# One layer of a streaming encoder: 64-row score products filled up to 128 rows, and a tile of the down projection split later

## The chip, the core and the metric

The kernel runs on one core of a Trainium2 chip. The metric is the device time of one execution in microseconds (us), as the median of several runs. The core has a matrix engine, TensorE (PE in the rows, its weight loads PEld), VectorE (DVE), ScalarE (ACT), GpSimd (POOL) and a queue (SP) that issues most of the DMAs. Each engine works through its own queue in order; semaphores tie the queues together.

## The reference, cut to what matters

512 positions of width 1024 go through one residual block: a normalised input is projected, eight heads of forgetting attention and eight latent heads of attention work on it, their outputs are gated, summed and projected, and a SwiGLU feed-forward part with 2816 hidden features and a last normalisation follow. The two places that matter here:

```python
def latent_attention(q_nope, q_rope, k_nope, k_rope, v):      # 8 heads, nope 64, rope 32, blocks of 128 queries
    s = (jnp.einsum('bqhd,bkhd->bhqk', qn, k_nope, preferred_element_type=jnp.float32)
         + jnp.einsum('bqhr,bkr->bhqk', qr, k_rope, preferred_element_type=jnp.float32))
    s = jnp.where(k_chunk[None, :] <= q_chunk[:, None], s * scale, NEG_INF)
    p = jax.nn.softmax(s, axis=-1).astype(v.dtype)
    return jnp.einsum('bhqk,bkhd->bqhd', p, v)

def swiglu(xn, w_gate, w_up, w_down):
    return (jax.nn.silu(xn @ w_gate) * (xn @ w_up)) @ w_down
```

## The kernel before

Every fp32 operand is held as two fp32r parts, a high and a low one (`split`, L98: ScalarE rounds to the high part, VectorE subtracts for the low part), and a product is made of three matmuls, high by high, high by low and low by high (`mm3`, L124). TensorE's own instructions are pinned in program order; the order of the other queues is set by a planner when the kernel is built (`schedule_with_timeline_sim`, L1042).

Attention runs over 64 items: for the latent heads ("b", tiles `hb`) and then the forgetting heads ("a", tiles `ha`), eight heads each, and for each head four blocks of 128 queries. The item of block i covers 128 (i + 1) keys, so the score products are 128, 256, 384 or 512 columns wide. The loop at L847 issues the scores three items ahead (`scores`, L641, tile `sp`); then come the maximum and the exponential (`softmax_a`, L653, tile `pe`), the scaling by the reciprocal of the sum (`softmax_b`, L663, L666 on VectorE), the transposes of the scaled block (`transpose`, L671, tile `pt`, then `pth` and `ptl`), and after the last item of a head the product with the values (`values`, tile `py`). Between these steps a `Filler` (L783) puts the matmuls of other jobs into TensorE's queue in a fixed list (L822): gate projections (`gates`, tile `pg`), the projections of later heads (`project_b`, tiles `pqb`, `pkb`; `project_a`, tile `pqa`), values (`pva`) and branch projections (`pb`). Each job that reads weights has them split just before (`whi` on ScalarE at L101, `wlo` on VectorE at L102).

`project_b(j)` (L566) makes the tiles of two latent heads. A head's tile `hd` has four planes of 128 rows by 512 positions. With `own` for the 64 rows of this head (rows 0 to 63 for even heads, 64 to 127 for odd ones) and `oth` for the other 64: plane 0 holds the query's high part in `own` and its low part in `oth`; plane 1 holds the key's high part in both halves; plane 2 holds the key's low part in `own`, and its other half is never written; plane 3 holds the rotary parts. The tiles come from a ring of 17 buffers (`u8`), so a later head's tile may have to wait until an earlier tile was read for the last time. Scores of a latent item are three matmuls into one bank: plane 0 by plane 1 over 128 rows (high by high and low by high at once), plane 0 by plane 2 over the 64 rows `own` (high by low, L650), and plane 3 by the shared rotary key `krs` over 100 rows. Scores of a forgetting item are two matmuls, over 128 and 70 rows.

GpSimd does the minimum in the gates (L435), a small copy into each `hb` tile (L590), and small memsets and DMAs for the `ha` tiles (L614 to L617).

The down projection (L955 on) has two halves of 512 output columns. In each half eleven strips of weights (256 hidden features, so two steps of 128 each) are added into one PSUM bank for each of the four tiles of 128 positions; the last three strips run tile by tile, so that the tail of one tile (adding the residual, squares, scaling, storing) runs beside the matmuls of the next. In the second half the last tile of positions is two parts of 256 columns in two banks, in all eleven strips.

Of the kernel before, what the change touches and what calls it, by code (L numbers as in the profile page):

```python
# [8 lines left out]
F32 = mybir.dt.float32  # L9
# [3 lines left out]
AF = mybir.ActivationFunctionType  # L13
ALU = mybir.AluOpType
AX = mybir.AxisListType

P = 128
D = 1024
S = 512
NT = S // P  # L20
# [4 lines left out]
NHC = HID // P  # L25
# [41 lines left out]
def tile_hybrid_fox_mla_block(  # L67
# [6 lines left out]
    nc = tc.nc  # L74
# [11 lines left out]
    def u8(shape, dtype, name):  # L86
        return big.tile(shape, dtype, name=name, tag="u8", bufs=17)

    def small(shape, name, dtype=F32, bufs=2):
        return big.tile(shape, dtype, name=name, tag=name, bufs=bufs)  # L90

    def tmp(shape, name, dtype=F32):
        return big.tile(shape, dtype, name=name, tag="p", bufs=4)

    def bank(tag, name):
        return ps.tile([P, 512], F32, name=name, tag=tag, bufs=3 if tag == "a" else 5)

    def split(hi, lo, src, scale=None):  # L98

        if scale is None:  # L100
            one = nc.scalar.copy(out=hi, in_=src)  # L101
            two = nc.vector.tensor_tensor(out=lo, in0=src, in1=hi.bitcast(F32), op=ALU.subtract)  # L102
        else:
            one = nc.scalar.activation(out=hi, in_=src, func=AF.Copy, scale=scale)
            two = nc.vector.scalar_tensor_tensor(out=lo, in0=src, scalar=scale, in1=hi.bitcast(F32),
                                                 op0=ALU.mult, op1=ALU.subtract)
        if pin[1]:
            tc.keep_in_program_order(one)
            tc.keep_in_program_order(two)
# [4 lines left out]
    def matmul(*args, **kw):  # L114
        ins = nc.tensor.matmul(*args, **kw)  # L115
        if pin[0]:
            tc.keep_in_program_order(ins)
# [6 lines left out]
    def mm3(o, a, b, start, stop):  # L124

        matmul(o, lhsT=a[0], rhs=b[0], start=start, stop=False)
        matmul(o, lhsT=a[0], rhs=b[1], start=False, stop=False)
        matmul(o, lhsT=a[1], rhs=b[0], start=False, stop=stop)

    def weights(src, a, b, spare=False):  # L130

        raw = big.tile([P, a, b], F32, name="wraw", tag="wr", bufs=2)
        nc.sync.dma_start(out=raw, in_=src)
        return split_weights(raw, spare)
# [23 lines left out]
    def mean4(out, ss, width):  # L158

        nc.vector.tensor_scalar(out=out, in0=ss, scalar1=-4.0 / width, scalar2=-4.0 * EPS, op0=ALU.mult, op1=ALU.add)  # L160

    def mean_rsqrt(parts, width, name, out=None):

        m = small([P, 1], name + "_m")
        mean4(m, parts[0], width)
        for p_ in parts[1:]:
            nc.vector.scalar_tensor_tensor(out=m, in0=p_, scalar=-4.0 / width, in1=m, op0=ALU.mult, op1=ALU.add)
        return rsqrt(m, 1, name, out)
# [17 lines left out]
    c1 = big.tile([P, C_INVF], F32, name="c1", tag="c1", bufs=1)  # L186
# [137 lines left out]
    for st in "f0 k0 f1 t0 k1 f2 t1 f3 t2 m1 t3 f4 t4 m2 t5 f5 f6 t6 f7 m3 t7 w0 w1".split():  # L324
        n = int(st[1])
# [50 lines left out]
    for n, (t, k, p_) in enumerate(jobs):  # L376
        if n == 72:
            token_rms()
        matmul(pms[t][:, :MISCW], lhsT=xt(k, slice(t * P, (t + 1) * P))[p_ == 2],
               rhs=(mh, ml)[p_ == 1][k // 4][:, k % 4, :], start=(k, p_) == (0, 0), stop=(k, p_) == (KC - 1, 2))  # L380
# [98 lines left out]
    def step():  # L479

        for _ in range(next(stages, 0)):
            next(pre, None)
# [41 lines left out]
    for t in range(NT):  # L524
        cols = slice(t * P, (t + 1) * P)
# [40 lines left out]
    def project_b(j):  # L566

        cols = slice(j * P, (j + 1) * P)
        two = [u8([P, 4, S], F32R, f"hb{2 * j + e}") for e in range(2)]
        pq = bank("b" if j == 0 else "a", "pqb")  # L570
        for k in range(2):
            mm3(pq, (qn[:, 0, k, cols], qn[:, 1, k, cols]), (cq[:, 0, k, :], cq[:, 1, k, :]), k == 0, k == 1)
            yield
        pk_ = bank("b" if j == 0 else "a", "pkb")
        mm3(pk_, (kvs[:, 2, cols], kvs[:, 3, cols]), (kvs[:, 0, :], kvs[:, 1, :]), True, True)
        yield
        if j == 0:
            rotated_to_features()
        for e in range(2):
            h = 2 * j + e  # L580
            hd = two[e]
            own, oth = slice(64 * e, 64 * e + 64), slice(64 - 64 * e, 128 - 64 * e)
            split(hd[own, 0, :], hd[oth, 0, :], pq[own, :], scale=SCALE_B)
            split(hd[own, 1, :], hd[own, 2, :], pk_[own, :])
            nc.scalar.copy(out=hd[oth, 1, :], in_=pk_[own, :])
            rows = slice(h % 4 * ROPE, (h % 4 + 1) * ROPE)
            nc.vector.tensor_copy(out=hd[0:32, 3, :], in_=qrh[h // 4][rows, :])
            nc.vector.tensor_copy(out=hd[32:64, 3, :], in_=qrl[h // 4][rows, :])
            nc.scalar.copy(out=hd[64:96, 3, :], in_=qrh[h // 4][rows, :])
            nc.gpsimd.tensor_copy(out=hd[96:100, 3, :], in_=qrow)  # L590
            heads["b", h] = hd
            yield
# [48 lines left out]
    def scores(it):  # L641
        b, h, W, qc = it.b, it.h, it.W, it.qc
        hd = heads[b, h]
        sp = it.sp = bank("b", "sp")
        matmul(sp[:, :W], lhsT=hd[:, 0, qc], rhs=hd[:, 1, :W], start=True, stop=False)
        if b == "a":
            matmul(sp[:, :W], lhsT=hd[0:70, 2, qc], rhs=hd[0:70, 3, :W], start=False, stop=True)
        else:
            own = slice(64 * (h % 2), 64 * (h % 2) + 64)
            matmul(sp[:, :W], lhsT=hd[own, 0, qc], rhs=hd[own, 2, :W], start=False, stop=False)  # L650
            matmul(sp[:, :W], lhsT=hd[0:100, 3, qc], rhs=krs[0:100, :W], start=False, stop=True)

    def softmax_a(it):  # L653
# [222 lines left out]
    gf = u8([P, 2, D], F32, "gf")  # L876
# [3 lines left out]
    def hrow(t):  # L880
        return ha[t // 2][:, t % 2, :]
# [9 lines left out]
    for half in range(2):  # L891
# [11 lines left out]
        for t in range(NT):  # L903
            po = bank("a", "po")
            cols = slice(t * P, (t + 1) * P)
# [7 lines left out]
            jk = tmp([P, S], "jk")  # L913
            nc.scalar.activation(out=jk, in_=hrow(t)[:, nn], func=AF.Square, accum_out=ssh[:, 2 * t + half:2 * t + half + 1])
            nc.vector.tensor_tensor(out=hn[t][:, nn], in0=hrow(t)[:, nn], in1=gf[:, 0, nn], op=ALU.mult)
            if half == 1:
                r = mean_rsqrt([ssh[:, 2 * t:2 * t + 1], ssh[:, 2 * t + 1:2 * t + 2]], D, "nh")
# [4 lines left out]
    act = [u8([P, 2, 2, S], F32R, f"act{i}") for i in range(NHC // 2)]  # L922
# [12 lines left out]
    for s in range(NHC // 2):  # L935
# [11 lines left out]
        for e in range(2):  # L947
            sg = tmp([P, S], "sg")
            last = nc.scalar.activation(out=sg, in_=pg[e], func=AF.Silu)
# [5 lines left out]
    ssf = small([P, 2 * NT + 1], "ssf", bufs=1)  # L955
    for half in range(2):
        nn = slice(half * 512, (half + 1) * 512)

        parts = [(t, 0, 512) for t in range(NT)]
        if half == 1:  # L960
            parts[-1:] = [(NT - 1, 0, 256), (NT - 1, 256, 512)]
        po = [bank("b" if half == 0 or t == NT - 1 else "a", "pd") for t, _, _ in parts]

        def step(s, e, n, w):
            t, c0, c1 = parts[n]
            cols = slice(t * P, (t + 1) * P)
            mm3(po[n][:, 0:c1 - c0], (act[s][:, e, 0, cols], act[s][:, e, 1, cols]),
                (w[0][:, e, c0:c1], w[1][:, e, c0:c1]), s == 0 and e == 0, s == NHC // 2 - 1 and e == 1)

        def load(s):  # L970
            return weights(w_ffn_down[s * 256:(s + 1) * 256, nn].rearrange("(k p) n -> p k n", p=P), 2, 512)

        last = 3
        for s in range(NHC // 2 - last):
            w = load(s)
            for e in range(2):
                for n in range(len(parts)):
                    step(s, e, n, w)
        ws = [(s, load(s)) for s in range(NHC // 2 - last, NHC // 2)]
        for n, (t, c0, c1) in enumerate(parts):  # L980
            for s, w in ws:
                for e in range(2):
                    step(s, e, n, w)
            cols = slice(half * 512 + c0, half * 512 + c1)
            hv = hrow(t)[:, cols]
            nc.vector.tensor_tensor(out=hv, in0=po[n][:, 0:c1 - c0], in1=hv, op=ALU.add)
            jk = tmp([P, S], "jk")
            at = 2 * t + half + (c0 > 0)
            nc.scalar.activation(out=jk[:, 0:c1 - c0], in_=hv, func=AF.Square, accum_out=ssf[:, at:at + 1])
            nc.vector.tensor_tensor(out=hv, in0=hv, in1=gf[:, 1, cols], op=ALU.mult)  # L990
            if half == 1 and c1 == 512:
                r = mean_rsqrt([ssf[:, i:i + 1] for i in range(2 * t, at + 1)], D, "nf")
                rows = slice(t * P, (t + 1) * P)
                h0, h1 = hrow(t)[:, 0:384], hrow(t)[:, 384:1024]
                nc.scalar.activation(out=h0, in_=h0, func=AF.Copy, scale=r)
                nc.vector.tensor_scalar(out=h1, in0=h1, scalar1=r, scalar2=None, op0=ALU.mult)
                nc.sync.dma_start(out=out2[rows, :], in_=hrow(t))
# [55 lines left out]
```

## Time and profile before

| | |
|---|---|
| median of 3 runs | 749.67 us (748.59 to 749.82) |
| profiled execution, time | 749.56 us |
| its span, first to last instruction | 747.8 us |
| TensorE busy | 730.3 us of the span |
| VectorE busy | 423.0 us |
| ScalarE busy | 335.9 us |
| GpSimd busy | 72.0 us |
| mean granted TensorE clock | 0.993 of full |
| latent scores, first to last start | 72.1 to 182.6 us |
| down projection, first to last matmul | 619.7 to 740.7 us |

The span is what the profiler saw from the first to the last instruction; the execution's time has 1.8 us around it. Busy time of TensorE counts matmuls that overlap, with ends that are modelled; what a matmul costs is read from the distance between the starts of one and the next. "idle before <-" names what ended an engine's idle time; "issue" is time in which the engine waited for nothing that the profile shows.

### The profile page before, as it was taken

To read this page: it belongs to the slowest core of one execution; us is meant where nothing else is said; L and a number is where in the kernel's file an instruction comes from. 1 tells how busy PE (TensorE), PEld (TensorE's weight loads), DVE (VectorE), ACT (ScalarE), POOL (GpSimd) and SP (SyncE) were. 2 spreads that over 40 slices of the span, in tenths; PEclk is the share of its full clock that TensorE was granted. 3 is DMA by queue.
4 is the path that set the end of the run, shared out by engine and by line. 5 is a ranking of instruction groups with operands and counts; after the bars stand their busy time and mean duration, and the time that the engine had idled before them with its cause. 6 is when DMAs were issued, how large, how long until landed. Compare 5 with 4: busy or idle time off the path is not lost.

```text
span 747.8 us, 9512 instructions
## 1 busy us (share of the span) xinstructions
PE 730.3 (98%) x3601; PEld 608.4 (81%) x3601; DVE 423.0 (57%) x818; ACT 335.9 (45%) x635; POOL 72.0 (10%) x88
## 2 busy tenths in 40 slices
PE   5999999999999999999999999999999999999996
PEld 3988777878888888887899888888888888888885
DVE  6998988666898986576644332333333233225214
ACT  7457977555675774534514232323232232213113
POOL 4242331012121020300000000000000000000000
PEclk9899999999999999999999999999999999999999
DMA  8512112131223222274302323333332323323212
GB/s 280 170 45 69 41 49 57 29 86 30 87 58 78 65 57 85 86 244 148 114 29 86 112 85 108 90 93 104 87 111 85 112 86 96 102 85 112 85 57 112
DMA packets 68941, 69.45 MB, mean 93 GB/s; under 512 B 3808, under 2 KB 58352, under 8 KB 68896
## 3 DMA queue, kind: packets, MB, share of 16 engines
q1 hardware_dynamic: 66240, 64.91, 29.3%
q10 hardware_dynamic: 1824, 3.38, 1.4%
q0 software_dynamic: 832, 0.57, 0.3%
q8 instruction: 28, 0.46, 0.2%
q14 instruction: 17, 0.14, 0.1%
HBM read 66.59 MB, written 2.10 MB: 92 GB/s over the span
## 4 chain that ended last, share of the span: by engine, by line
PE 90%; DVE 4%; ACT 2%; DMA 2%; issue 1%; SPq 0%
PE pg L115 26%; PE pd L115 16%; PE pu L115 16%; PE pqa L115 6%; PE pb L115 6%; PE sp L115 4%; PE po L115 4%; PE pva L115 3%; PE py L115 3%; PE pt L120 2%; PE pm L115 2%; DMA wraw<-in_w_out_dram 1%; DMA wraw<-in_w_in_dram 1%; PE pqb L115 1%; ACT sq L340 1%
## 5 line engine op out<-in xcount | busy, mean ns | idle before, releaser
L102 DVE TENSOR_TENSOR wlo<-wraw,whi 128x1024 fp32r<-128x1024 f32 x102 | 125.4, 1230 | 200.6 <-ACT whi L101 200.1
L101 ACT CAST whi<-wraw 128x1024 fp32r<-128x1024 f32 x102 | 106.8, 1048 | 214.4 <-PE pu L115 78.5
L115 PE MATMUL pd<-whi,act 128*128 128x512 f32 (+1 forms) x396 | 110.9, 366 | 0.0
L115 PEld LDWEIGHTS pd<-whi,act 128*128 128x128 f32 x396 | 71.6, 189 | 12.4
L115 PE MATMUL pd<-wlo,act 128*128 128x512 f32 (+1 forms) x198 | 72.5, 366 | 0.0
L115 PE MATMUL pg<-hTh,wlo 128*128 128x512 f32 (+1 forms) x192 | 71.4, 372 | 0.0
L115 PE MATMUL pu<-hTl,whi 128*128 128x512 f32 (+1 forms) x192 | 71.3, 371 | 0.0
L115 PE MATMUL pu<-hTh,whi 128*128 128x512 f32 (+1 forms) x192 | 71.3, 371 | 0.0
L115 PE MATMUL pu<-hTh,wlo 128*128 128x512 f32 (+1 forms) x192 | 71.3, 371 | 0.0
L115 PE MATMUL pg<-hTl,whi 128*128 128x512 f32 (+1 forms) x192 | 71.3, 371 | 0.0
L115 PE MATMUL pg<-hTh,whi 128*128 128x512 f32 (+1 forms) x192 | 71.1, 371 | 0.0
L115 PE MATMUL pg<-xTh,whi 128*128 128x512 f32 x128 | 52.4, 410 | 0.0
L115 PE MATMUL pg<-xTh,wlo 128*128 128x512 f32 x128 | 50.2, 392 | 0.0
L115 PE MATMUL pg<-xTl,whi 128*128 128x512 f32 x128 | 50.1, 391 | 0.0
L115 PEld LDWEIGHTS pd<-wlo,act 128*128 128x128 f32 x198 | 37.4, 189 | 6.1
L115 PEld LDWEIGHTS pu<-hTh,wlo 128*128 128x128 f32 x192 | 36.2, 188 | 6.3
L115 PEld LDWEIGHTS pg<-hTh,wlo 128*128 128x128 f32 x192 | 36.2, 188 | 6.3
L115 PEld LDWEIGHTS pu<-hTl,whi 128*128 128x128 f32 x192 | 36.2, 188 | 6.3
L115 PEld LDWEIGHTS pg<-hTl,whi 128*128 128x128 f32 x192 | 36.2, 188 | 6.2
L115 PEld LDWEIGHTS pg<-hTh,whi 128*128 128x128 f32 x192 | 36.2, 188 | 6.2
L115 PEld LDWEIGHTS pu<-hTh,whi 128*128 128x128 f32 x192 | 36.2, 188 | 6.1
L435 POOL TENSOR_SCALAR gate<-gate 128x512 f32<-128x512 f32 x16 | 28.2, 1762 | 116.8 <-ACT gate L433 116.5
(281 smaller groups left out, 1433.7 us busy)
## 6 DMA issues: line engine op xcount, KB each, us to landing
wraw<-in_w_in_dram SPq DMA_DIRECT2D x28, 512.0 KB, 3.9
wraw<-in_w_ffn_gate_dram SPq DMA_DIRECT2D x22, 512.0 KB, 3.7
wraw<-in_w_ffn_up_dram SPq DMA_DIRECT2D x22, 512.0 KB, 3.7
wraw<-in_w_ffn_down_dram SPq DMA_DIRECT2D x22, 512.0 KB, 3.7
wraw<-in_w_out_dram SPq DMA_DIRECT2D x8, 512.0 KB, 4.0
xf<-in_xT_dram SPq DMA_DIRECT2D x8, 256.0 KB, 5.1
wraw<-in_w_branch_b_dram SPq DMA_DIRECT2D x4, 512.0 KB, 3.5
wraw<-in_w_branch_a_dram SPq DMA_DIRECT2D x4, 512.0 KB, 3.3
```

Source lines behind the costliest of these rows:

```text
L101: one = nc.scalar.copy(out=hi, in_=src)
L102: two = nc.vector.tensor_tensor(out=lo, in0=src, in1=hi.bitcast(F32), op=ALU.subtract)
L115: ins = nc.tensor.matmul(*args, **kw)
L120: ins = nc.tensor.transpose(*args)
L340: tc.keep_in_program_order(nc.scalar.activation(out=dst, in_=src, func=AF.Square))
L435: nc.gpsimd.tensor_scalar(out=g, in0=g, scalar1=1e30, scalar2=None, op0=ALU.min)
```

## The change

The unused half of plane 2 of each latent head's tile is set to zero by GpSimd, and the second score product runs over all 128 rows instead of 64: the added rows multiply the query's low part by zero. In the down projection's second half, the last tile of positions is one bank of 512 columns for the first eight strips. In the last three strips columns 0 to 255 go on in that bank, and then columns 256 to 511 of these three strips are added up in a new bank, `late`. The first bank's columns 256 to 511 are added to the residual by an instruction of its own, and the new bank's columns after it. All other tiles do what they did.

```diff
@@ project_b
             split(hd[own, 0, :], hd[oth, 0, :], pq[own, :], scale=SCALE_B)
+
+            nc.gpsimd.memset(hd[oth, 2, :].bitcast(F32), 0.0)
             split(hd[own, 1, :], hd[own, 2, :], pk_[own, :])
@@ scores
         else:
-            own = slice(64 * (h % 2), 64 * (h % 2) + 64)
-            matmul(sp[:, :W], lhsT=hd[own, 0, qc], rhs=hd[own, 2, :W], start=False, stop=False)
+            matmul(sp[:, :W], lhsT=hd[:, 0, qc], rhs=hd[:, 2, :W], start=False, stop=False)
             matmul(sp[:, :W], lhsT=hd[0:100, 3, qc], rhs=krs[0:100, :W], start=False, stop=True)
@@ down projection
-        parts = [(t, 0, 512) for t in range(NT)]
-        if half == 1:
-            parts[-1:] = [(NT - 1, 0, 256), (NT - 1, 256, 512)]
-        po = [bank("b" if half == 0 or t == NT - 1 else "a", "pd") for t, _, _ in parts]
+        po = [bank("b" if half == 0 or t == NT - 1 else "a", "pd") for t in range(NT)]
...
+        for s in range(NS - last):
             w = load(s)
             for e in range(2):
-                for n in range(len(parts)):
-                    step(s, e, n, w)
+                for t in range(NT):
+                    step(po[t], s, e, t, w, 0, 512, s == 0 and e == 0, False)
+        ws = [(s, load(s)) for s in range(NS - last, NS)]
+        for t in range(NT):
+            if half == 1 and t == NT - 1:
+
+                for s, w in ws:
+                    for e in range(2):
+                        step(po[t][:, 0:256], s, e, t, w, 0, 256, False, s == NS - 1 and e == 1)
+                late = bank("b", "pd")
+                for s, w in ws:
+                    for e in range(2):
+                        step(late[:, 0:256], s, e, t, w, 256, 512, s == NS - last and e == 0, s == NS - 1 and e == 1)
+                add(t, po[t][:, 0:256], 0, 256, 2 * t + 1)
+                hv = hrow(t)[:, 768:1024]
+                nc.vector.tensor_tensor(out=hv, in0=po[t][:, 256:512], in1=hv, op=ALU.add)
+                add(t, late[:, 0:256], 256, 512, 2 * t + 2)
+            else:
+                for s, w in ws:
+                    for e in range(2):
+                        step(po[t], s, e, t, w, 0, 512, False, s == NS - 1 and e == 1)
+                add(t, po[t], 0, 512, 2 * t + half)
```

`add` is the old tail of a part as a function: the residual's addition on VectorE, the squares on ScalarE with their sum, and the multiplication by the last gain on VectorE. The scaling and the store behind it are as before.

## Rows read from the trace of the kernel before

**Rows 1.** Windows: stretch; busy us and instructions of each engine; clock, DMA
```profile
88.40:121.00 32.60, 32.60 (x152) 24.45 (x153) 29.18 (x67) 27.20 (x61) 10.33 (x12) 1.00 0.16 43
121.00:186.00 65.00, 65.00 (x389) 54.20 (x389) 44.51 (x97) 37.10 (x84) 7.16 (x15) 1.00 0.20 54
```
**Rows 2.** Chain that ended last, in time, latent heads: start us, us, what
```profile
88.40 0.41 PE pt L120 x2
...
90.20 0.74 PE sp L115 x3
...
91.97 0.92 PE sp L115 x3
...
95.42 1.09 PE sp L115 x3
...
100.66 0.57 PE sp L115 x3
...
181.99 1.08 PE sp L115 x3
```
**Rows 3.** The same chain, forgetting heads
```profile
199.36 0.17 PE sp L115 x2
...
201.88 0.24 PE sp L115 x2
...
204.56 0.35 PE sp L115 x2
...
207.41 0.46 PE sp L115 x2
```
**Rows 4.** Timeline, weight loads of one latent item: start, us, instruction [idle before]
```profile
138.04 0.18 PEld L115 LDWEIGHTS sp<-hb 64*128 64x128 f32 x1 [0.24 <-issue]
...
138.46 0.19 PEld L115 LDWEIGHTS sp<-krs,hb 100*128 100x128 f32 x1 [0.24 <-issue]
```
**Rows 5.** Timeline of VectorE, 94 to 111 us
```profile
95.37 0.69 DVE L102 TENSOR_TENSOR ptl<-pt,pth 128x512 fp32r<-128x512 f32 x1 [0.57 <-ACT pth L101]
...
96.55 0.42 DVE L587 CAST hb<-qr 32x512 fp32r<-32x512 f32 x1 [0.22 <-PE sp L115]
96.97 0.74 DVE L588 CAST hb<-qr 32x512 fp32r<-32x512 f32 x1
...
101.69 0.16 DVE L665 RECIPROCAL rs<-sm 128x1 f32<-128x1 f32 x1 [1.50 <-ACT pe L661]
...
110.79 0.27 DVE L666 TENSOR_SCALAR pe<-pe,rs 128x128 f32<-128x128 f32 x1
```
**Rows 6.** Timeline: who is ready just before TensorE asks
```profile
111.20 0.30 PE L120 MATMUL pt<-c,pe 128*128 128x128 f32 x1
...
134.62 1.22 DVE L102 TENSOR_TENSOR wlo<-wraw,whi 128x1024 fp32r<-128x1024 f32 x1
...
135.96 0.28 PE L115 MATMUL pva<-wlo,xTh 128*128 128x256 f32 x1
```
**Rows 7.** GpSimd's groups by line: count | busy us, mean ns | idle before
```profile
L614 POOL MEMSET ha<- 6x512 f32 x8 | 4.2, 527 | 69.3 <-PE sp L115 56.9 <-PE py L115 11.4 <-DVE hb L588 0.9
```
**Rows 8.** Timeline of GpSimd
```profile
91.21 1.50 POOL L435 TENSOR_SCALAR gate<-gate 128x512 f32<-128x512 f32 x1 [3.13 <-ACT gate L433]
96.64 0.79 POOL L590 CAST hb<-yfa 4x512 fp32r<-4x512 f32 x1 [3.94 <-PE sp L115]
```
**Rows 9.** Timeline, down projection: every third matmul (`wlo`) of 512 and 256 columns
```profile
734.04 0.39 PE L115 MATMUL pd<-wlo,act 128*128 128x512 f32 x1
...
734.72 0.39 PE L115 MATMUL pd<-wlo,act 128*128 128x512 f32 x1
...
738.09 0.28 PE L115 MATMUL pd<-wlo,act 128*128 128x256 f32 x1
...
738.45 0.28 PE L115 MATMUL pd<-wlo,act 128*128 128x256 f32 x1
```
**Rows 10.** Timeline, the tail
```profile
740.44 0.55 DVE L996 TENSOR_SCALAR ha<-ha,nf_r 128x640 f32<-128x640 f32 x1
...
741.04 0.42 DVE L986 TENSOR_TENSOR ha<-pd,ha 128x256 f32<-128x256 f32 x1
...
743.49 0.62 ACT L995 ACTIVATE ha<-ha,nf_r 128x384 f32<-128x384 f32 x1 [0.48 <-DVE nf_r L155]
```

More of the change, by code (lines that the diff above doesn't have):

```diff
@@ L957, in tile_hybrid_fox_mla_block, with step @@
         nn = slice(half * 512, (half + 1) * 512)
-        parts = [(t, 0, 512) for t in range(NT)]
-        if half == 1:
-            parts[-1:] = [(NT - 1, 0, 256), (NT - 1, 256, 512)]
-        po = [bank("b" if half == 0 or t == NT - 1 else "a", "pd") for t, _, _ in parts]
-        def step(s, e, n, w):
-            t, c0, c1 = parts[n]
+        po = [bank("b" if half == 0 or t == NT - 1 else "a", "pd") for t in range(NT)]
+        def step(o, s, e, t, w, c0, c1, start, stop):
             cols = slice(t * P, (t + 1) * P)
-            mm3(po[n][:, 0:c1 - c0], (act[s][:, e, 0, cols], act[s][:, e, 1, cols]),
-                (w[0][:, e, c0:c1], w[1][:, e, c0:c1]), s == 0 and e == 0, s == NHC // 2 - 1 and e == 1)
+            mm3(o, (act[s][:, e, 0, cols], act[s][:, e, 1, cols]), (w[0][:, e, c0:c1], w[1][:, e, c0:c1]), start, stop)
@@ L970, in load, with add @@
         def load(s):
             return weights(w_ffn_down[s * 256:(s + 1) * 256, nn].rearrange("(k p) n -> p k n", p=P), 2, 512)
+        def add(t, o, c0, c1, at):
+            cols = slice(half * 512 + c0, half * 512 + c1)
+            hv = hrow(t)[:, cols]
+            nc.vector.tensor_tensor(out=hv, in0=o, in1=hv, op=ALU.add)
+            jk = tmp([P, S], "jk")
+            nc.scalar.activation(out=jk[:, 0:c1 - c0], in_=hv, func=AF.Square, accum_out=ssf[:, at:at + 1])
+            nc.vector.tensor_tensor(out=hv, in0=hv, in1=gf[:, 1, cols], op=ALU.mult)
@@ L973, in tile_hybrid_fox_mla_block @@
+        NS = NHC // 2
         last = 3
-        for s in range(NHC // 2 - last):
+        for s in range(NS - last):
             w = load(s)
             for e in range(2):
-                for n in range(len(parts)):
-                    step(s, e, n, w)
[L979 to L992, printed above, removed]
+                for t in range(NT):
+                    step(po[t], s, e, t, w, 0, 512, s == 0 and e == 0, False)
@@ new lines, in tile_hybrid_fox_mla_block @@
+        ws = [(s, load(s)) for s in range(NS - last, NS)]
[17 more added lines that the diff above has]
+                add(t, po[t], 0, 512, 2 * t + half)
+            if half == 1:
+                r = mean_rsqrt([ssf[:, i:i + 1] for i in range(2 * t, 2 * t + (3 if t == NT - 1 else 2))], D, "nf")
```

## The prediction

> **What bounds the kernel now.** I read the windows first, then the chain of waits, then the timeline at the places that the chain names. From 88.40 to 186 us TensorE is busy in every microsecond, at full clock [rows 1]; the chain enters it at 88.40 with the second item's transposes, which had waited for VectorE, and stays on it to the last latent score block [rows 2]. So from there each nanosecond that a score block occupies TensorE is on the path. Before 88.40 the chain runs over VectorE and ScalarE, with TensorE only just ahead. The windows also say where TensorE is alone: from 121 to 186 us VectorE is busy 44.51 of 65.00 us, but from 88.40 to 121 it is busy 29.18 of 32.60, about 90% [rows 1]. There it is a second bound, close behind.
>
> **What a score block costs, and why.** Three products of a latent item take 0.57, 0.74, 0.92 and 1.09 us for 128, 256, 384 and 512 columns [rows 2]. The forgetting heads give the price without a 64-row product: two products, of 128 and 70 rows, take 0.17, 0.24, 0.35 and 0.46 us [rows 3], that is 0.085, 0.12, 0.175 and 0.23 each; three would take 0.26, 0.36, 0.525 and 0.69. The excess is 0.31, 0.38, 0.395 and 0.40 us, nearly the same at every width, so it is a fixed stop and not work. The timeline shows where it sits: the load of the 64-row weights begins late, with 0.24 us idle before it, and so does the 100-row load behind it, another 0.24 [rows 4]; nothing that the profile knows was being waited for. The array is emptied when it goes to 64 rows and again when it goes back. Products of 70 and 100 rows show that it is not the missing rows as such: 70 behind 128 costs nothing extra [rows 3]. A zero-filled product over 128 rows should therefore run as the first one does, and both stops go. Per head that is 0.31 + 0.38 + 0.395 + 0.40 = 1.485 us.
>
> **Which of it reaches the end.** There are 32 blocks. Five are issued before 88.40, where VectorE sets the pace: counted at nothing, since TensorE would only wait longer for the transposes at 88.40. Of the other 27 (six of 128, seven of each other width) the full sum is 6 x 0.31 + 7 x (0.38 + 0.395 + 0.40) = 10.09 us.
>
> The next seven (0.38 + 0.395 + 0.40, then 0.31 + 0.38 + 0.395 + 0.40 = 2.66 us) lie before the transpose at 111.20. Its input is scaled by VectorE from 110.79 for 0.27 us [rows 5], so it was ready 0.14 us ahead [rows 6]. VectorE has few holes on the way there that an earlier TensorE could close: 0.57 us (behind ScalarE's cast of a transposed block) and 0.22 (behind a score block); the 1.50 us at 101.69 hang on ScalarE, which was itself behind VectorE [rows 5]. So VectorE can come forward by 0.57 + 0.22 = 0.79, and of the 2.66 us I count 0.79. After it, five heads' worth of blocks (the 20 from the thirteenth on) give 5 x 1.485 = 7.43; VectorE has room there, and scaled blocks are mostly ready microseconds early. Two places are tight: weights' low part done at 134.62 + 1.22 = 135.84 and used at 135.96, 0.12 ahead, with a block of 384 columns in the loop [rows 6], which gives back 0.395 - 0.12 = 0.28; and a like pair near 172 us with 0.10 and a 128-column block, 0.21. Scores: 0.79 + 7.43 - 0.49 = 7.73 us.
>
> **The memsets.** Eight, of 64 x 512 elements, on GpSimd. The trace has memsets of 6 x 512 at 0.527 us [rows 7] and a 4 x 512 copy at 0.79 [rows 8]; since the length of a row and not the number of rows should count, I take 0.53 and keep 0.79 as the upper end. GpSimd is busy 10.33 of 32.60 us in the fuller stretch [rows 1], so 8 x 0.53 = 4.2 us fit, and the tiles are read later. What may not be free is VectorE: its copy of 32 x 512 at 96.97 took 0.74 us beside GpSimd's copy of 96.64, the one just before it 0.42 [rows 5, 8]. A memset that meets such a copy would cost 0.32 us on the engine that is the bound until 121 us. All eight memsets fall before 121; bounds 0 and 8 x 0.32 = 2.56. I take a third, 0.85, about the chance of GpSimd's present work to meet any one of VectorE's instructions (10.33 of 32.60). A gain from the memset itself is excluded: it only adds.
>
> The Trainium skill ("SBUF — State Buffer", section on two separate sides) says that VectorE and GpSimd share one port pair, that whoever has it keeps it for a whole instruction and the other stops. By that, a memset that comes first would stop a copy for up to its own length, and eight would cost up to 4.2 us by the length above; the sum below would end near 745.6. No row here has a memset beside such a copy.
>
> The added wait: a memset has to wait until its tile is free, as GpSimd's copy for one head waited 3.94 us for a score block [rows 8]. Behind it in GpSimd's queue stand that copy and the gates' minimum (L435), and behind the minimum ScalarE's next step. With the memset placed where the copy stands, nothing new waits: the hole of 3.94 us was there.
>
> **The down projection.** Matmuls of 512 columns start (734.72 - 734.04) / 3 = 0.227 us apart, those of 256 (738.45 - 738.09) / 3 = 0.120 [rows 9]. Eight strips of two steps of three products, 48 in all, change from two of 256 to one of 512: 48 x (0.240 - 0.227) = 0.64 us off TensorE's path, which is the chain up to 741 us. The last three strips cost what they did. Added is one VectorE addition of 256 columns, 0.42 us, in the last 2.1 us before the final one; VectorE finished the third tile's scaling at 740.44 + 0.55 = 740.99, only 0.05 before its last addition at 741.04 [rows 10]. If the new one falls in a small hole it costs nothing, else up to 0.42; I take 0.2. Net gain 0.44, bounds 0.22 and 0.64. The tail after 741.04 (to 743.49 + 0.62) stays [rows 10].
>
> **Sum.** 749.56 - 7.73 + 0.85 - 0.44 = 742.2 us against the profiled execution, whose time lies 0.11 under the median; so 742.3.
>
> **Rivals.**
> *All of it arrives.* The planner may set VectorE's queue differently, so that the scaling at 110.79 comes earlier; then 10.09 + 0.64 come off, 738.9, and with the five early blocks (0.31 + 0.38 + 0.395 + 0.40 + 0.31 = 1.80) 737.1. For it: scaled blocks elsewhere wait microseconds. Against: VectorE is at 90%, and most of that work is needed in that stretch.
> *The stop is not the row count.* If the load of the second product is late for another reason (it takes its weights from the same plane as the first, say), the filled product stops too, and only the down projection gains: 749.67 - 0.4 = 749.2. Against: two products without a stop at 70 rows [rows 3]. The Trainium skill ("TensorE: Matmul & The Clock Gate", section on packing small matmuls) says that a weight load overlaps running matmuls only where its group of rows differs from theirs; by that, a 128-row load would be the one to wait, and this rival would hold. The loads of 100 and 64 rows in rows 4 are the late ones, so the trace speaks against it.
> *Slower: a memset in front of a gate.* If the planner puts the memset of a tile that is still read ahead of the minimum at 91.21, that minimum and ScalarE's queue behind it wait to 96.5, 5.3 us [rows 8]. Two heads take over a tile so late; at both places 10.6 us, against 7.3 of gain: 749.7 + 3.3 = 753.0. It decides where the memset stands ahead of the minimum in GpSimd's queue; one such place alone still leaves a gain.
> *A small gain.* All memsets meet copies (2.56) and VectorE comes forward by nothing: 749.67 - (7.43 - 0.98) + 2.56 - 0.44 = 745.3, with the tight places counted twice.
>
> **How the numbers follow.** The forecast (739.9 to 746.0) gets 0.66, all of it 0.20, not the row count 0.06, slower 0.05, and a gain between 746.0 and 748.2 from further waits 0.03. The range 738.0 to 746.0 takes in the forecast and most of the full gain. A difference of 0.2%, 1.5 us, is about what a measurement of this kernel can tell from none. Faster 0.66 + 0.20 + 0.03 = 0.89, same 0.06, slower 0.05.
>
> **What would show it.** Latent score blocks in the chain at 0.26, 0.36, 0.53 and 0.69 us, and no idle "issue" before score loads. New waits of TensorE for VectorE's scaling near 88 and 110 us, of some 2 us each. The forgetting stretch as long as before. Copies at L587 and L588 of 0.4 or 0.7 us beside memsets. 594 matmuls of `pd` become 546, in about 120.3 us. Wrong it would be with score blocks as long as before, or with GpSimd holding a gate.

## The result and the profile after

The changed kernel takes 741.27 us, the median of four runs (740.01 to 742.44), against 749.13 us for the kernel before in the same comparison (748.59 to 749.82): a ratio of 0.9894, interval 0.987 to 0.9918. The forecast was 742.3. The profiled execution took 740.01 us, that of before 749.56. Its span is 738.20 us against 747.78, 9.58 us less.

Where the 9.58 us went is read by setting the same instructions of the two chains side by side. The first is the chain of waits of the kernel after; columns as in [rows 2].

```profile
88.37 0.41 PE pt L120 x2
...
90.18 0.35 PE sp L115 x3
...
91.56 0.53 PE sp L115 x3
...
94.60 0.70 PE sp L115 x3
...
110.31 0.21 DVE pe L667
...
110.65 0.30 PE pt L120
...
112.94 0.28 PE sp L115 x3
...
174.51 0.70 PE sp L115 x3
...
199.55 0.47 PE sp L115 x2
...
324.66 5.27 DMA wraw<-in_w_out_dram
...
611.52 119.92 PE pd L115 x546
```

The same two late entries in the chain of the kernel before:

```profile
332.59 5.96 DMA wraw<-in_w_out_dram
...
620.12 120.90 PE pd L115 x594
```

Three products of a latent item now take 0.28, 0.35, 0.53 and 0.70 us (112.94, 90.18, 91.56, 94.60), against 0.57, 0.74, 0.92 and 1.09 [rows 2]. The stop is gone at every width. A two-product block of the forgetting heads is what it was, 0.47 against 0.46 [rows 3].

The landmarks give the sum. The second item's transposes start at 88.37, against 88.40: nothing won up to there. The transpose that stood at 111.20 [rows 6] stands at 110.65: 0.55 won, and what it waits for is VectorE's scaling at 110.31. The last latent block ends at 174.51 + 0.70 = 175.21, against 181.99 + 1.08 = 183.07: 7.86 won, 7.31 of it in the five heads after 110.65. The wait for the output weights' transfer is 0.69 shorter. The down projection's chain is 119.92 us long against 120.90: 0.98. Together 7.86 + 0.69 + 0.98 = 9.53, and 0.05 is spread over the rest.

The waits of TensorE in the kernel after: engine, tile and line, what it waited for, us in total, times, longest.

```profile
PE pt L120 <- DVE pe L667: 2.9, 2, 2.0
...
PE sp L115 <- DVE rs L666: 0.9, 1, 0.9
```

The two waits at `pt` are the ones near 88 and 110 us: 2.0 us at 88.37, where the kernel before waited 0.4, and 0.9 at 110.65. The wait at `sp`, 0.9 us at 107.48, is new too; the profile puts it down to VectorE's reciprocal (L666). TensorE gets its score blocks done earlier and then stands before VectorE. The windows of the kernel after (columns as in [rows 1]) show the two regimes:

```profile
88.40:111.00 22.60, 20.82 (x107) 17.07 (x108) 20.62 (x46) 18.27 (x42) 8.82 (x12) 1.00 0.18 48
121.00:180.00 59.00, 59.00 (x395) 54.25 (x394) 44.25 (x97) 37.59 (x87) 6.61 (x14) 1.00 0.21 56
```

Up to 111 us VectorE is busy 20.62 of 22.60 us, 91%, and TensorE has 1.78 us without work. From 121 us on TensorE is still without a hole, in a stretch that has become shorter. There nearly every nanosecond taken from a block was a nanosecond of the kernel: 7.31 us of the 7.43 that the blocks of five heads had to give.

The memsets and VectorE's copies, in the kernel after: by line, engine, count, ns min/median/max, first and last start, form.

```profile
L589 DVE CAST hb<-qr x8: 404/432/735, 64.3 to 107.4; 32x512 fp32r<-32x512 f32 x8
L590 DVE CAST hb<-qr x8: 418/733/740, 66.2 to 107.9; 32x512 fp32r<-32x512 f32 x8
```

The same two lines in the kernel before, where they are L587 and L588:

```profile
L587 DVE CAST hb<-qr x8: 405/417/858, 64.4 to 107.5; 32x512 fp32r<-32x512 f32 x8
L588 DVE CAST hb<-qr x8: 417/419/744, 66.3 to 108.4; 32x512 fp32r<-32x512 f32 x8
```

The median of the second copy went from 0.42 to 0.73 us. GpSimd now does a memset (L585) and then its own copy (L592), and one of the two runs when VectorE's second copy starts in five of eight cases (in a sixth it is the gates' minimum, as before). One such pair, VectorE's two copies in the chain and GpSimd's two instructions in the timeline of the kernel after:

```profile
103.67 0.70 DVE hb L589
104.39 0.73 DVE hb L590
```

```profile
103.57 0.52 POOL L585 MEMSET hb<- 64x512 f32 x1
104.15 0.69 POOL L592 CAST hb<-yfa 4x512 fp32r<-4x512 f32 x1
```

The memset ends at 104.09, and the copy of VectorE that began beside it at 104.37. GpSimd's copy ends at 104.84, and VectorE's second copy at 105.12. Both times VectorE ends 0.28 us behind GpSimd, so its copy is held until GpSimd's instruction is done. All 16 copies together took 9.36 us, against 8.51 in the kernel before: 0.85 more.

The tail, VectorE in the kernel after: start, us, instruction.

```profile
729.67 0.42 DVE L997 TENSOR_TENSOR ha<-pd,ha 128x256 f32<-128x256 f32 x1
...
730.86 0.55 DVE L1009 TENSOR_SCALAR ha<-ha,nf_r 128x640 f32<-128x640 f32 x1
731.46 0.42 DVE L972 TENSOR_TENSOR ha<-pd,ha 128x256 f32<-128x256 f32 x1
```

The added addition (L997) starts at 729.67, and the scaling of the third tile ends at 730.86 + 0.55 = 731.41, 0.05 before the last addition. That is the same margin as before (740.99 against 741.04, [rows 10]): the addition fell into a hole.

### The profile page after: what moved, and what is told of

The parts are those of the page before. It is cut to its first block, busy times and chain, and to the rows that moved or that the text cites. A ratio compares the mean times of both kernels' runs of the same rounds, so it can differ in the third digit from the quotient of the medians.

```text
span 738.2 us, 9427 instructions
## 1 busy us (share of the span) xinstructions
PE 719.0 (97%) x3553; PEld 605.8 (82%) x3553; DVE 423.2 (57%) x819; ACT 335.4 (45%) x635; POOL 75.7 (10%) x96
## 4 chain that ended last, share of the span: by engine, by line
PE 87%; DVE 6%; ACT 2%; DMA 2%; issue 2%; SPq 0%; ACTq 0%; DVEq 0%
PE pg L115 26%; PE pu L115 16%; PE pd L115 16%; PE pqa L115 6%; PE pb L115 6%; PE po L115 4%; PE pva L115 3%; PE sp L115 3%; PE py L115 3%; PE pt L120 2%; DMA wraw<-in_w_out_dram 1%; DMA wraw<-in_w_in_dram 1%; PE ptr L120 0%; DVE wol L102 0%; ACT xTh L104 0%
## 5 line engine op out<-in xcount | busy, mean ns | idle before, releaser
L115 PE MATMUL pd<-whi,act 128*128 128x512 f32 (+1 forms) x364 | 109.2, 382 | 0.0
L115 PEld LDWEIGHTS pd<-whi,act 128*128 128x128 f32 x364 | 67.6, 188 | 13.2
L115 PE MATMUL pd<-wlo,act 128*128 128x512 f32 (+1 forms) x182 | 69.5, 382 | 0.0
L115 PEld LDWEIGHTS pd<-wlo,act 128*128 128x128 f32 x182 | 34.2, 188 | 6.7
```

## The experiments

All are changes of the kernel before or the kernel after, and all are compared with runs of the kernel before on the same chip.

**The two parts, each alone.** First the scores alone:

```diff
 kernel before, and only
+            nc.gpsimd.memset(hd[oth, 2, :].bitcast(F32), 0.0)
-            own = slice(64 * (h % 2), 64 * (h % 2) + 64)
-            matmul(sp[:, :W], lhsT=hd[own, 0, qc], rhs=hd[own, 2, :W], ...)
+            matmul(sp[:, :W], lhsT=hd[:, 0, qc], rhs=hd[:, 2, :W], ...)
```

> The kernel before with the first part of the change alone (memsets and 128-row second products); the down projection is as before. Theory (the stop at the 64-row product goes; VectorE lets little of it through before 111 us): the changed kernel's profile ended its latent scores 7.9 us earlier and its down projection was 0.98 us shorter, so about 749.1 - 7.9 + 1.0 = 742.2 us, and blocks of 0.28, 0.35, 0.53 and 0.70 us. Rival (the down projection brought a good part): 744 or more.

Measured: 742.43 us, ratio 0.9916 (0.9902 to 0.993), so 6.55 us of gain.

```diff
 kernel after, and the scores as before
-            nc.gpsimd.memset(hd[oth, 2, :].bitcast(F32), 0.0)
-            matmul(sp[:, :W], lhsT=hd[:, 0, qc], rhs=hd[:, 2, :W], ...)
+            own = slice(64 * (h % 2), 64 * (h % 2) + 64)
+            matmul(sp[:, :W], lhsT=hd[own, 0, qc], rhs=hd[own, 2, :W], ...)
```

> The kernel before with the second part alone: the last tile is split only in the last three strips; score products of 64 rows as before. Theory (48 products of 512 columns for 96 of 256, on TensorE's path): between 0.64 us off, as the prediction counted, and 0.98, the difference of the two profiles; about 748.3. Rival (the added addition on VectorE delays the tail by 0.2 to 0.4): 748.6 to 749.1.

Measured: 747.85 us, ratio 0.9987 (0.9978 to 0.9997), 1.13 us of gain; the chain over `pd` is 119.92 us long there too, 0.98 less than before. 6.55 + 1.13 = 7.68 against 7.86 for both: within their intervals the parts add up. In this kernel the wait for the output weights is 5.30 us, as in the kernel after, though nothing of its scores was changed, while with the scores alone it is 6.03. So the 0.69 us of that wait in the account above don't come from the score edit. Whether they come with the down projection's edit stays open: the same transfer took 5.59 to 6.03 us in the four profiles without that edit, and 5.27 to 5.71 in seven of the eight with it, but 6.04 in the eighth, and each kernel was profiled once.

**Is it the row count?** Even heads get 96 rows (32 of them zero), odd heads keep 64, in one kernel:

```diff
 kernel before, and
+            if e == 0:
+                nc.gpsimd.memset(hd[64:96, 2, :].bitcast(F32), 0.0)
-            matmul(sp[:, :W], lhsT=hd[own, 0, qc], rhs=hd[own, 2, :W], ...)
+            if h % 2 == 0:
+                matmul(sp[:, :W], lhsT=hd[0:96, 0, qc], rhs=hd[0:96, 2, :W], ...)
+            else:
+                matmul(sp[:, :W], lhsT=hd[64:128, 0, qc], rhs=hd[64:128, 2, :W], ...)
```

> The kernel before, with the second product of the even latent heads over rows 0 to 95 (32 rows zeroed) and that of the odd heads over their 64 rows as before. Theory (the array stops when it goes to 64 rows and back, and not at 96, as it does not at 70 or 100): even heads' blocks 0.28, 0.35, 0.53, 0.70 us, odd heads' 0.57, 0.74, 0.92, 1.08; half of the 16 later blocks' and of the first's gain, 745.3 to 746. Rival (any product narrower than the 128-row one before it stops): even heads' blocks stay at 0.57 to 1.08 and the time at 749.

Measured: 745.33 us, ratio 0.9958 (0.9944 to 0.9972). The chain of this kernel, an odd head's four blocks, then an even head's, then the next odd head's first:

```profile
112.59 0.57 PE sp L115 x3
116.21 0.74 PE sp L115 x3
119.37 0.91 PE sp L115 x3
122.80 1.09 PE sp L115 x3
127.36 0.28 PE sp L115 x3
129.98 0.36 PE sp L115 x3
132.78 0.53 PE sp L115 x3
135.90 0.71 PE sp L115 x3
140.50 0.57 PE sp L115 x3
```

With 96 rows a block takes 0.28, 0.36, 0.53 and 0.71 us, with 64 rows 0.57, 0.74, 0.91 and 1.09, a few microseconds apart in one execution. That settles it. The rival in which the product stops for another reason, its weights from the same plane as the first one's, falls: the 96-row product takes them from the same plane too. Nor does it matter which 64 rows they are: in the kernel before, the even heads' products stop as the odd heads' do. It need not be 128 rows either; with 70, 96 and 100 rows there is no stop. The Trainium skill ("TensorEngine Tiling (Array Packing)", Key Properties) says that changing the tiling mode drains TensorE; the trace agrees, with the stops at a change between 64 rows and more. The Trainium skill's sentence on weight loads that spoke for the rival (in "TensorE: Matmul & The Clock Gate", cited in the prediction) would have the 128-row loads wait; the trace speaks against it, with three products of a block in 0.70 us, 0.23 each, where the load of each lasts 0.19.

**The stop by itself, where nothing else is near.** In the feed-forward stage TensorE is alone on the path. At ten places between strips 16 products of 256 columns are added, into a bank that nobody reads, so the output is unchanged. They alternate between 128 and 64 rows in the first kernel, and all have 128 in the second:

```diff
 kernel after, and for ten strips
+            px = bank("a", "px")
+            for k in range(8):
+                a, b_ = ht(k, slice(0, P)), ht(k, slice(0, 256))
+                matmul(px[:, 0:256], lhsT=a[0], rhs=b_[0], start=True, stop=True)
+                matmul(px[:, 0:256], lhsT=a[0][0:64], rhs=b_[0][0:64], start=True, stop=True)
 second kernel: [0:128] in place of [0:64]
```

> The changed kernel with 16 products more in each of ten strips of the feed-forward part, into a bank that nobody reads: eight of 128 rows by 256 columns, each followed by one of 64 rows. Theory (the array is emptied when it goes to 64 rows and when it goes back, about 0.19 us each way at any width): 160 products of 0.12 us and 160 stops of 0.19: 19.2 + 30.4 = 50 us above the changed kernel, some 790. If the planner sets them apart between other products, as many stops.

> The same 160 products with all of them over 128 rows. Theory: 160 x 0.12 = 19.2 us above the changed kernel, 760, so 30 us below the run with 64 rows. Rival (a stop comes from the same weights' plane or the same bank being used again, not from the rows): as long as the run with 64 rows.

Measured: 814.38 us with alternating rows, 760.34 with 128 rows throughout. The second is as expected: 160 products more, 19.1 us over the kernel after, 0.119 each. The first is 54 us dearer, where 160 stops of 0.19 us would make 30. The chain of the alternating kernel around one such place:

```profile
404.57 5.64 PE px L115 x16
410.22 13.25 PE pu L115 x48
...
434.35 5.04 PE px L115 x16
```

and of the kernel with 128 rows throughout:

```profile
405.76 1.91 PE px L115 x16
407.68 10.91 PE pu L115 x48
```

At full clock the products start 0.31 us apart, from 128 rows to 64 and from 64 back to 128, where products of one kind start 0.12 apart. So the stop is 0.19 us each way, and a 64-row product among 128-row ones costs twice that, 0.38, as the score blocks of 256 columns and more had it. But at the place shown first the 16 products took 5.64 us instead of 16 x 0.31 = 5.0, and the strip behind them 13.25 instead of 10.9. The windows of the alternating kernel say why (columns as in [rows 1]; the eighth value, behind the five engines, is the granted clock):

```profile
404.00:408.00 4.00, 4.00 (x15) 2.37 (x13) 1.23 (x1) 1.97 (x3) 0.00 (x0) 0.99 0.17 47
408.00:414.60 6.60, 6.60 (x16) 4.64 (x16) 0.00 (x0) 0.00 (x0) 0.00 (x0) 0.50 0.26 76
```

From 408.0 to 414.6 us the granted clock was 0.50, the lower of its two levels (1.2 GHz). Before it fell TensorE had waited for no other engine; it had only stopped between products. This came at all ten places, for 3.4 or 6.8 us each, 54.4 us together. Half of that, 27 us, is an estimate of the work lost, and it is about the remaining 24 us (54 - 30). Both kernels ran once; the differences are many times what runs of one kernel differ by.

**What the memsets cost.** The memsets without anything that reads them:

```diff
 kernel before, and only
+            nc.gpsimd.memset(hd[oth, 2, :].bitcast(F32), 0.0)
```

> The kernel before with the eight memsets alone; the 64-row products don't read what they write. Theory (GpSimd has room; VectorE's copies beside it may last longer): 0 to 0.85 us above the kernel before, 749.1 to 750.0. Rival (shared port: each memset stops a copy of VectorE on the chain): up to 2.6 us, 751.7.

Measured: 751.01 us, ratio 1.0021 (1.0008 to 1.0033): 2.0 us, with an interval of 0.6 to 2.5. In its profile the time between the transposes at 88 and at 111 us grew by 0.86, and L590 took 0.73 us at the median, as in the kernel after. VectorE's 16 copies together took 10.30 us there, 1.79 more than in the kernel before. So the memsets do cost something where VectorE is the bound. The interval holds the forecast's 0.85 and ends just short of the 2.56 of all eight colliding: the median lies nearer to the second, and the runs don't rule out the first. With the memsets in both kernels, the 128 rows are worth 751.01 - 742.43 = 8.58 us.

Next, the memsets as soon as the two tiles are taken, where they were meant to meet no copy:

```diff
 kernel after, without its memset, and right behind the two tiles of a pair
+        for e in range(2):
+            nc.gpsimd.memset(two[e][64 - 64 * e:128 - 64 * e, 2, :].bitcast(F32), 0.0)
```

> The changed kernel, with the two memsets of a pair of heads put where the pair's tiles are taken, ahead of its projections. Theory (the memsets alone cost the kernel before some 2 us, because VectorE's copies stand beside them at 0.73 us instead of 0.42): memsets that run in GpSimd's idle stretches no longer meet them, at least for the first four heads: 739.5 to 740.5 beside 741.3, and the median of L590's copies back towards 0.42 us. Rival (the copies are held by GpSimd's own small copies that follow, which stay): 741 to 742. The other rival: a memset that waits for its tile holds the gates' minimum behind it, 743 or more.

Measured: 740.44 us, ratio 0.9888 (0.9874 to 0.9902). The memsets of this kernel in its timeline, and the third of the kernel after beside them:

```profile
42.41 1.09 POOL L571 MEMSET hb<- 64x512 f32 x2
...
76.69 0.52 POOL L571 MEMSET hb<- 64x512 f32 x1
```

```profile
76.47 0.69 POOL L585 MEMSET hb<- 64x512 f32 x1
```

Only the first pair of memsets ran early. The other six start within 0.31 us of where they start in the kernel after, each still just ahead of GpSimd's own copy. The copies of this kernel:

```profile
L589 DVE CAST hb<-qr x8: 415/418/694, 65.6 to 107.7; 32x512 fp32r<-32x512 f32 x8
L590 DVE CAST hb<-qr x8: 417/498/744, 67.4 to 108.2; 32x512 fp32r<-32x512 f32 x8
```

Together they took 8.39 us, 0.97 less than in the kernel after, but 0.62 of that was won by the first four, before 69 us. The transpose that stood at 110.65 starts at 111.00, no earlier, and the time can't be told from that of the kernel after. So the collisions that are gone, most of them before 69 us, are not what the end waited for. What the six memsets that stayed cost with the faster scores was not tested.

**Is VectorE the bound before 111 us?** If so, work taken off it should bring the transposes forward. One of its two copies per head goes to GpSimd, then both:

```diff
 kernel after, and
-            nc.vector.tensor_copy(out=hd[32:64, 3, :], in_=...)
+            nc.gpsimd.tensor_copy(out=hd[32:64, 3, :], in_=...)
 second kernel: hd[0:32, 3, :] too
```

> The changed kernel, with one of VectorE's two copies for each latent head (L590, 32 x 512, 0.42 us, or 0.73 beside GpSimd) given to GpSimd. Theory (until 111 us VectorE is the bound, and gives out time there one for one): 8 x 0.42 to 0.73 us leave it, of which TensorE can use the 2 us that it now waits near 110 and part of the 0.9 to 2 near 88: 738.5 to 740.5 beside 741.3 of the changed kernel. Rival (GpSimd's copies hold VectorE as long as they last, about 0.6 us each): no gain, 741 to 742.5.

Measured: 736.7 us, ratio 0.9837 (0.982 to 0.9854), 4.6 us under the kernel after. The transposes, in its chain:

```profile
86.71 0.41 PE pt L120 x2
...
107.72 0.30 PE pt L120
```

They start 1.66 and 2.93 us earlier than in the kernel after. GpSimd takes 0.61 us for the copy at the median, and VectorE has eight copies less. Profile against profile the gain is 740.01 - 736.91 = 3.1 us, nearly all of it these 2.93.

> The changed kernel, with both of VectorE's copies for each latent head given to GpSimd. Theory: up to twice as much leaves VectorE, and no copy of VectorE is left beside GpSimd's work; TensorE's waits near 88 and 110 us go, 738 to 740. Rival: GpSimd, with 8 x 3 more instructions of some 0.6 us in the same stretch, becomes late for the gates' minimum or the heads' tiles: 742 or more.

Measured: 740.0 us, ratio 0.9878 (0.9859 to 0.9896): all of it lost again. In its chain GpSimd stands in VectorE's place:

```profile
78.44 0.52 POOL hb L585
78.96 0.55 POOL hb L589
...
79.55 0.61 POOL hb L590
...
80.20 0.61 POOL hb L592
```

Four of GpSimd's instructions per head in a row hold the latent heads, and the transposes are back at 88.28 and 110.64. For the second of these GpSimd isn't the only cause: in the windows of this kernel the granted clock is at half just behind the first.

```profile
89.40:92.90 3.50, 3.50 (x13) 2.86 (x13) 3.40 (x8) 2.46 (x7) 1.49 (x1) 0.51 0.16 30
```

Of the 2.92 us lost at the second transpose, 1.57 were lost at the first (88.28 against 86.71), before the clock fell. How much of the rest each of the two makes stays open.

Last, the better of the two with the early memsets, of which again only the first pair runs early:

```diff
 one copy on GpSimd (as above), and the early memsets (as above)
```

> The same with one of VectorE's two copies on GpSimd as well (the run that took 736.7 us). Theory: another 0.5 to 1 us off, 735.7 to 736.2. Rival: 736.5 to 737.5, or over 738 if a gate is held.

Measured: 736.46 us, ratio 0.9834 (0.982 to 0.9848), the fastest of all, though not to be told from 736.7. It beats both kernels.

## Why the prediction was right, by its steps

**What bounds the kernel** held. VectorE paces it to 111 us, as the windows after and the copy on GpSimd show. Behind that TensorE does, as the 7.31 us show that came through in full from there.

**The stop.** Its cause (64 rows after 128 and back) and its size were read rightly; 96 rows in one half of the heads and the alternating products settled it. Blocks were forecast at 0.26, 0.36, 0.53 and 0.69 us and came at 0.28, 0.35, 0.53 and 0.70.

**The five first blocks, counted at nothing,** gave 0.03. **The seven before 111.20** gave 0.55, where 0.79 was counted for them and up to 0.85 for the memsets against them. VectorE's copies from 88 to 111 us took 0.47 us longer in sum than before, but what the blocks and the memsets each did to the 0.55 can't be taken apart in this execution. The rival *all of it arrives* failed at this point: TensorE waits for the scaling at the two places named, 2.0 and 0.9 us, where the prediction had said some 2 us each.

**The 20 blocks after it** gave 7.31 of 7.43. The step that failed is the 0.49 us for two tight places: only 0.12 is missing. The timeline of the kernel after shows the first of them, the split of the weights and the matmul that was to wait for it:

```profile
132.00 1.22 DVE L102 TENSOR_TENSOR wlo<-wraw,whi 128x1024 fp32r<-128x1024 f32 x1
```

```profile
132.88 0.28 PE L115 MATMUL pva<-wlo,xTh 128*128 128x256 f32 x1
```

The matmul starts at 132.88, before the split ends at 133.22, so it reads weights that were split earlier, and the 0.12 us of [rows 6] were no margin. At the second place it is the same: the split ends at 165.98, and the matmul starts at 165.79. Where the 0.12 us went stays open.

**The memsets** were forecast at 0.85, as a third of the eight collisions possible, and VectorE's copies grew by 0.85 us in the kernel after. That the two agree to this digit is luck: with the memsets alone the copies grew by 1.79 and the kernel by 2.0 (0.6 to 2.5). Four of the eight second copies in the kernel after are held by GpSimd's own copy, which now comes behind the memset; the prediction had counted the memset alone. The price of one collision was read rightly, 0.73 instead of 0.42. The Trainium skill's rule that the prediction weighed ("SBUF — State Buffer", section on two separate sides) would have VectorE's copy stop until the memset is done; the trace agrees. In all profiles together 75 of VectorE's copies started while a memset into these tiles or GpSimd's copies into them ran; 73 ended 0.27 to 0.28 us after that instruction, and the other two, which had under 0.1 us of it left, took their usual 0.42. The 4.2 us that the prediction worked out from the rule were an upper end: in the kernel after the memsets held five copies, each for what was left of the memset, and made them 1.1 us longer in all.

**The down projection** brought 0.98 in the profile and 1.13 alone, where 0.44 was forecast, with an upper bound of 0.64. Two terms were mis-sized. The added addition cost nothing instead of 0.2. And the mean distance of two 512-column matmuls outside the 256-column groups fell from 227.7 to 226.7 ns, since some of the first five behind such a group had taken 231 to 236. Of 594 matmuls 132 had 256 columns before, so 462 had 512; 462 x 0.001 = 0.46 us at most, and 0.98 - 0.64 = 0.34 was missing. The prediction had priced the 256-column groups and not the 512-column matmuls behind them.

**The rest,** 0.69 us at the output weights, is a transfer that no term of the prediction covers. It isn't the scores' doing, as the second experiment shows; whether it comes with the down projection's edit or differs from execution to execution stays open.

So the forecast was 1.0 us above the median and 2.2 above the profiled execution, where the working is: scores and memsets together gave 7.86 where 6.88 was forecast (0.98), the down projection 0.54 more than forecast, and the transfer 0.69. Between profile and median lies the spread of the kernel after: two of its runs took 740.01 and 740.24, two 742.30 and 742.44, and the mean granted clock was 0.994 in the profiled one of the first pair and at most 0.991 in the second. What the clock did in the second pair isn't recorded in time. A like event is, in the profiled execution of the scores alone, which took 744.49 us:

```profile
84.00:89.60 5.60, 3.59 (x18) 2.64 (x16) 5.39 (x12) 4.82 (x12) 1.96 (x4) 1.00 0.04 6
89.60:93.20 3.60, 3.57 (x12) 3.02 (x13) 3.37 (x10) 3.18 (x8) 0.75 (x1) 0.53 0.03 5
```

From 84.0 to 89.6 us TensorE was busy 3.59 of 5.60 us; from 89.6 to 93.2 its granted clock was 0.53, nearly all of it at the lower level. That loses about 3.6 x 0.47 = 1.7 us of work at full clock, an estimate, and fits the 2.2 us between the two pairs. That the pairs differ by this is argued, not shown.

## What to carry over

Set the duration of a group of small matmuls against the sum of its parts, taken from groups elsewhere in the same trace: a fixed excess at every width is a stop, and a product of 64 rows among products of 128 costs two of them (0.38 us here), more than the work that zeros add. Then count the saving only where TensorE is the bound, and where it isn't, take work off the engine that is: 2.66 us of score blocks bought 0.55 us in VectorE's stretch, while one line of small copies moved to GpSimd bought 2.9 there. Moving too much turns the helper into the bound. And look in the trace whether what was moved in the code has moved on the engine: of the eight early memsets six had not.

## What the runs showed of the hardware that was not expected

The granted clock fell to 0.50 in a stretch in which TensorE waited for no other engine and only changed between 128 and 64 rows (0.31 us from start to start for products of 256 columns instead of 0.12); in all ten places, with about 24 us of 814 lost to it. Alternating heights cost twice, by the stops and by the clock behind them.

A memset of 64 x 512 elements took GpSimd 0.52 us, as one of 6 x 512 does [rows 7]: the number of rows didn't count.

A copy of 32 x 512 took VectorE 0.42 us alone. Started while GpSimd ran a memset or a small copy, it ended 0.28 us after that instruction, however much was left of it, so that it took 0.43 to 0.85 us. The gates' minimum did not always hold it: at 75.53 in the kernel after, with 0.88 us of the minimum left, the copy took 0.42, and the next, with 0.46 left, 0.73. GpSimd did the same copy in 0.61.
